# Hybrid trunk kernel: selection and adaLN steps held back during the spatial gating, and another block order in the first layer's attention

## The chip, the cores and the metric

One core of a Trainium2 chip runs the whole kernel. The metric is the device time of one execution in microseconds. All times below are of the kernel before; the trace is that of one profiled execution.

## The reference

Two layers of a decoder trunk for one sequence of 1024 tokens with a width of 1024. Each layer normalises its input and modulates it by adaLN, multiplies it by one wide input matrix, and splits the product: u, v and z_a feed a spatial gating unit (group A), q, k, val and z_b a sparse attention (group B), and q_idx, k_idx and w_idx an indexer that scores which 256 keys each query may see.

```
def hybrid_layer(x, cond, cos, sin, w_ada, ...):
    mod = cond @ w_ada + b_ada
    shift, scale, gate = jnp.split(mod, 3, axis=-1)
    h = layer_norm(x) * (1.0 + scale[:, None, :]) + shift[:, None, :]
    proj = h @ w_in
    u, v, z_a, q, k, val, z_b, q_idx, k_idx, w_idx = jnp.split(proj, SPLIT_POINTS, axis=-1)
    y_a = jax.nn.silu(z_a) * spatial_gating_unit(u, v, v_norm_g, v_norm_b, w_spatial, b_spatial)
    # rope on q, k, q_idx, k_idx
    y_b = jax.nn.silu(z_b) * sparse_attention(q, k, val, q_idx, k_idx, w_idx)
    y = jnp.concatenate([y_a, y_b], axis=-1) @ w_out
    return layer_norm(ALPHA * x + gate[:, None, :] * y, ln_g, ln_b)

def spatial_gating_unit(u, v, g_v, b_v, w_s, b_s):      # chunks of 128 tokens, 8 groups
    vn = layer_norm(v, g_v, b_v)
    mixed = einsum('gts,bcsgd->bctgd', causal(w_s), vn) + b_s
    return u * mixed

def block(i):                                           # sparse attention, 128 queries
    score = sum over heads of w_idx * relu(q_idx . k_idx), causal
    idx = top_k(score, 256)
    p = softmax(q . k[idx] * scale), valid keys only
    return p @ v[idx]
```

## The kernel before

**Numbers and tiles.** All is float32. A matmul is done as three: each operand is split into a high and a low part, and high x high, low x high and high x low are summed in PSUM. Tokens lie in eight blocks of 128 (0 to 7), and in two halves of 512 (blocks 0 to 3 and 4 to 7). A scheduler sorts the instructions of each engine beforehand: what is written earlier in the program has priority, and later work that is ready fills gaps. So each engine runs a fixed row of instructions, and the order in which generators are advanced in the code sets where they stand in it.

**A layer, in the order of the code.** `layer` (L876 on) projects keys and values and the first half of the indexer's queries, and then goes through a list of weight pairs, n = 0 to 10 (L883 to L889): the indexer's second pair of queries, two pairs of v, two of q, and then u and z_a twice each, and two of z_b. The projections are L349. `halves` (L882) says which half of the tokens is projected first: blocks 0 to 3, or blocks 4 to 7 where the layer before treated a block from 4 up first.

**Behind n = 0** the indexer's scores of blocks 2 to 7 are made (L528 to L538, the last addition being the causal mask L538), and `select` is put into the list of generators (L935). It finds for each row of a block the threshold of the 256 best by bisection: statistics of the scores (L556, L557), then six rounds. A round counts the scores over a threshold for six blocks (L543, six counts with 384 to 1024 columns), and updates the bounds with some ten small operations (L584 to L600). Behind the rounds stand a sum on TensorE (L606), a flag, a branch that is hardly ever taken (L612), and per block the masks (L621 to L629). Blocks 0 and 1 need no selection.

**Behind n = 2** comes the spatial gating `sgu` (L468): for each of eight chunks four transposes of v (L474), its statistics (L234, L236, L238, and a power on GpSimd, L239), the norm (L243), a product with the spatial weights (L442) into the single PSUM buffer "o", and four operations on DVE (L480) that add the bias and write the result. Later u is multiplied on (L492) straight from the projection's PSUM buffer "acc", of which there are two.

**Side work.** `side()` (L910 to L920) is called between the pieces of the projections (from n = 1) and between the chunks of the gating (L938). Each call adds PACE_SEL to one account and PACE to another; for each whole unit the first advances `select` by one step, the second, from n = BACK on, one step of the next layer's adaLN (`ada_step`). Such a step is for instance a scaled addition of 128 rows of the adaLN matrix on DVE (L199; the first of a sum is L197); its sum is closed by matmuls with ones (L213, L223) and additions on DVE (L215, L224). For n under BACK no step is made by side(). What is left when the list is through is drained (L940).

**The attention** (L948 to L999) goes over sixteen steps: each block in the order of ORDERS and each of two groups of four heads. `att_soft` makes scores (L678), adds the mask and finds the maximum on DVE (L679), then exponentials on ScalarE (L684), a reciprocal (L686) and a product on GpSimd (L687). `att_pv` transposes the probabilities (L698), splits them (L701 on ScalarE, L702 on DVE) and multiplies by v (L703, L704) into "o"; L710 and L712 apply the gate. A block's length grows with its number: block 7 has 8 key blocks, block 0 has one. Between the steps the output projection (L740) is filled in: for the order's positions in MERGE both halves of a block's output at once (`merge_top`), for others group A's half ahead (`out_top`) and group B's after (`out_bottom`). The next layer's rows are normalised, transposed (L272) and loaded there, in the attention's order; those of the last blocks behind it (L1000 to L1008). MERGE and TOPS speak of positions in the order, not of block numbers.

Of the kernel before, what the change touches and what calls it, by code (L numbers as in the profile page):

```python
# [66 lines left out]
class Trunk:  # L67
    BUFS = dict(h=16, ya=4, wr=2, w=6, r=6, kd=2, vv=1, q=2, ga=6, gb=3, gc=4)
    PBUFS = dict(acc=2, s=2, pt=3, o=1)
    PACE_SEL = 0.8  # L70
    STEPS = 6
    PTAGS = ('ya', 'w', 'w', 'ya', 'w')
    ORDERS = ((1, 0, 2, 3, 4, 5, 6, 7), (4, 5, 6, 2, 3, 7, 1, 0))
    PACE = 1.1
    RDVE = 1
    DMOD = ()
    RT = 2
    XK = (0, 4, 4, 7)
    H0 = 10
    BACK = 5  # L80
    ADAE = (1, 1, 1)
    ADA0 = 0
    ADA1 = 0
# [678 lines left out]
    def bottom_split(self, l, A):  # L762
        A["r"] = self.load_row(self.xin[l] if self.ORDERS[l].index(A["i"]) in self.MERGE[l] else self.r_dram[l], A["i"])
        A["ys"] = self.g("gc", [P, 4, P], F32R), self.g("gc", [P, 4, P], F32R)
        self.split(A["ys"][0], A["ys"][1], A["y"])
# [8 lines left out]
    def out_bottom(self, l, A, w, end):  # L774
        nc = self.nc
        i, r = A["i"], A["r"]
        for nh in range(2):
            acc = yield from self.out_mm(w, A["ys"], nh, A["acc"][nh])
            rv = r[:, nh * 512:(nh + 1) * 512]
            if self.ORDERS[l].index(i) in self.MERGE[l]:  # L780
                nc.vector.scalar_tensor_tensor(rv, rv, ALPHA, acc, op0=ALU.mult, op1=ALU.add)  # L781
# [94 lines left out]
    def layer(self, l, wts):  # L876
# [4 lines left out]
        self.ya = []  # L881
        self.halves = (0, 1) if l == 0 or self.ORDERS[l - 1][0] < 4 else (1, 0)  # L882
        specs = [(C_QI + 256, True, lambda w: self.queries(l, 1, 1, w))]  # L883
# [11 lines left out]
        def ada_step(k):  # L895
            while k and back:
                if next(back[0], 1):
                    back.pop(0)
                else:
                    k -= 1  # L900
# [9 lines left out]
        def side():  # L910
            owed[0] += self.PACE_SEL
            while owed[0] >= 1:
                owed[0] -= 1
                for g in gens:
                    next(g, None)
            owed[1] += self.PACE
            while owed[1] >= 1:
                owed[1] -= 1
                if n >= self.BACK:
                    ada_step(1)  # L920

        w = self.load_pair(l, specs[0][0], specs[0][1])
        for n, (c0, rope, f) in enumerate(specs):
            nw = self.load_pair(l, specs[n + 1][0], specs[n + 1][1]) if n + 1 < len(specs) else None
            for _ in f(w):
                if n:
                    side()
                if n < self.BACK:
                    ada_step(self.ADA1)
            w = nw  # L930
            if n == 0:
                for i in range(2, NB):
                    masks[i] = self.t(f"sc{i}", [P, (i + 1) * P])
                    self.drain(self.scores(l, i, masks[i]))
                gens.append(self.select(masks, range(2, NB)))  # L935
                self.sgu_setup(l)
            if n == 2:
                for _ in self.sgu(l):  # L938
                    side()
        for g in gens + back:  # L940
            self.drain(g)
        wt, wb = [], []
# [4 lines left out]
        nc.sync.dma_start(self.lb, a["ln_b"][l].partition_broadcast(P))  # L947
        order = self.ORDERS[l]  # L948
        steps = [(i, g) for i in order for g in range(2)]
# [111 lines left out]
```

## Time and profile before

| | |
|---|---|
| median of 3 runs | 1205.03 us (1204.15 to 1211.92) |
| profiled execution | 1208.58 us |
| its span | 1206.9 us, mean granted TensorE clock 0.969 |
| TensorE | 1122.7 us busy (93%), 5460 instructions |
| weight loads | 892.3 us (74%), beside TensorE |
| DVE | 842.1 us (70%), 1900 |
| ScalarE | 502.2 us (42%), 972 |
| GpSimd | 554.7 us (46%), 469 |

Times count from the first instruction of the profiled execution. A row of the waits says which instruction TensorE stood before, who ended the idle time, its sum, its number and the longest. A busy time over a stretch counts only what lies within. In a timeline a run of equal instructions stands in one row with its count, and what it waited for in brackets. The clock is the share of full speed (2.4 GHz) that was granted, mean over a stretch; 0.5 is 1.2 GHz.

### The profile page before, as it was taken

The numbers are of one execution on the slowest core, as the hardware profiler recorded it, in microseconds if no ns is written. First come the engines' busy times: TensorE is split into PE (matmuls) and PEld (weight loads), VectorE is DVE, ScalarE is ACT, GpSimd is POOL, SyncE is SP. The second block draws the span as 40 slices with busy tenths as digits, with TensorE's granted clock in tenths as the row PEclk, the third lists the DMA queues.
The fourth block names the chain that finished last, engine by engine and source line by source line (L and its number), as shares of the span: only waits on it lengthen the run. The fifth ranks groups of instructions, "written<-read, shape, count | busy, mean of one in ns | idle before, by whom it ended". The sixth has DMA issues, their size and how long they took to land. (4 is left out here: it accounts for less than half of the span.)

```text
span 1206.9 us, 16501 instructions
## 1 busy us (share of the span) xinstructions
PE 1122.7 (93%) x5460; PEld 892.3 (74%) x5460; DVE 842.1 (70%) x1900; ACT 502.2 (42%) x972; POOL 554.7 (46%) x469
## 2 busy tenths in 40 slices
PE   5889999997999989988988999999989998999997
PEld 1467788866878778866766787888677886787885
DVE  6775666999773355688985467589977127878775
ACT  0342355420202454465764435562211136667561
POOL 1563310553323495474766532126323357565653
PEclk9989999998899989999999999999989998999999
DMA  8935721567412574322232474222621246132311
GB/s 264 278 101 179 205 71 36 166 219 257 117 54 79 166 218 158 105 97 62 86 95 74 138 229 123 70 68 88 227 90 45 88 132 202 51 106 88 114 36 61
DMA packets 127057, 152.11 MB, mean 126 GB/s; under 512 B 17396, under 2 KB 94580, under 8 KB 126968
## 3 DMA queue, kind: packets, MB, share of 16 engines
q1 hardware_dynamic: 126968, 151.03, 40.4%
q8 instruction: 43, 0.70, 0.2%
q14 instruction: 46, 0.38, 0.1%
HBM read 111.40 MB, written 35.40 MB: 122 GB/s over the span
## 5 line engine op out<-in xcount | busy, mean ns | idle before, releaser
L349 PE MATMUL pacc<-h,w 128*128 128x512 f32 (+2 forms) x2304 | 548.5, 394 | 10.8 <-DVE ya L492 8.4
L349 PEld LDWEIGHTS pacc<-h,w 128*128 128x128 f32 (+1 forms) x2304 | 427.1, 190 | 106.8 <-DVE ya L492 10.1
L303 POOL TENSOR_TENSOR w<-wr,w 128x512 fp32r<-128x512 f32 (+1 forms) x100 | 133.0, 1345 | 247.7 <-ACT w L302 231.9
L740 PE MATMUL pacc<-h,gc 128*128 128x512 f32 x768 | 196.7, 401 | 10.8 <-ACT gc L302 10.8
L740 PEld LDWEIGHTS pacc<-h,gc 128*128 128x128 f32 x768 | 143.8, 192 | 40.0 <-ACT gc L302 11.9
L302 ACT ACTIVATE w<-wr 128x512 fp32r<-128x512 f32 (+1 forms) x100 | 56.4, 601 | 208.9 <-PE pacc L349 147.0
L535 DVE SCALAR_TENSOR_TENSOR sc<-gc,wi,sc 128x384 f32<-128x384 f32 (+3 forms) x140 | 99.3, 752 | 38.8 <-ACT gc L530 37.0
L678 PE MATMUL ps<-kd,q 128*128 128x512 f32 (+4 forms) x384 | 106.2, 377 | 9.1 <-DVE mx L679 8.8
L702 DVE TENSOR_TENSOR ga<-ppt,ga 128x512 fp32r<-128x512 f32 x144 | 96.6, 684 | 15.5 <-ACT ga L701 14.9
L701 ACT ACTIVATE ga<-ppt 128x512 fp32r<-128x512 f32 x144 | 82.4, 592 | 36.8 <-PE ppt L698 35.9
L368 POOL TENSOR_TENSOR ga<-ga,ga 128x512 fp32r<-128x512 f32 (+2 forms) x40 | 56.9, 1429 | 85.5 <-ACT ga L367 76.8
L678 PEld LDWEIGHTS ps<-kd,q 128*128 128x128 f32 x384 | 65.1, 196 | 26.7 <-DVE mx L679 19.5
L687 POOL TENSOR_SCALAR w<-w,rd 128x256 f32<-128x256 f32 (+6 forms) x77 | 61.3, 799 | 50.7 <-DVE rd L686 32.5
L698 PE MATMUL ppt<-ident,w 128*128 128x128 f32 x349 | 74.9, 276 | 0.0
L239 POOL TENSOR_TENSOR rs<-rs,mhalf 128x1 f32<-128x1 f32 x48 | 34.8, 730 | 81.2 <-DVE rs L238 81.2
L722 DVE TENSOR_TENSOR wr<-wr,r 128x1024 f32<-128x1024 f32 x8 | 12.1, 1508 | 84.6 <-DMA wr<-in_w_out 52.3
L684 ACT ACTIVATE w<-w,mx 128x256 f32<-128x256 f32 (+6 forms) x77 | 60.6, 787 | 23.4 <-DVE mx L679 23.1
L703 PE MATMUL po<-ga,vv 128*128 128x512 f32 x144 | 62.4, 433 | 8.5 <-DVE gb L710 6.7
L543 DVE TENSOR_SCALAR_CACHE_REDUCE junkd<-sc,sv 128x384 int8<-128x384 f32 (+2 forms) x72 | 67.7, 940 | 1.4
L704 PE MATMUL po<-ga,vv 128*128 128x512 f32 x144 | 63.2, 439 | 3.0 <-DVE ga L702 2.9
L530 ACT ACTIVATE gc<-ppt 128x384 f32<-128x384 f32 (+3 forms) x96 | 47.9, 526 | 30.4 <-PE ppt L528 25.8
L199 DVE SCALAR_TENSOR_TENSOR r<-r,cond,r 128x1024 f32<-128x1024 f32 x28 | 41.8, 1494 | 25.4 <-DMA r<-in_w_ada 25.4
(198 smaller groups left out, 1750.5 us busy)
## 6 DMA issues: line engine op xcount, KB each, us to landing
wr<-in_w_in SPq DMA_DIRECT2D x50, 512.0 KB, 4.7
r<-in_w_ada SPq DMA_DIRECT2D x32, 512.0 KB, 4.2
q<-q SPq DMA_DIRECT2D x112, 128.0 KB, 3.2
q<-ga SPq DMA_DIRECT2D x48, 256.0 KB, 3.0
h<-in_w_ada SPq DMA_DIRECT2D x32, 256.0 KB, 5.2
wr<-in_w_out SPq DMA_DIRECT2D x16, 512.0 KB, 4.1
r<-r SPq DMA_DIRECT2D x14, 512.0 KB, 3.9
r<-x SPq DMA_DIRECT2D x12, 512.0 KB, 4.8
```

Of the source, the lines that this page charges most:

```text
L303: self.nc.gpsimd.tensor_tensor(lo, src, hi.bitcast(F32), op=ALU.subtract)
L349: self.nc.tensor.matmul(acc[:m, :tn], w[:, k, :m], h[:, k % 2, t0:t0 + tn], start=(k == 0 and i == 0), stop=(k == NK - 1 and i == 2))
L535: nc.vector.scalar_tensor_tensor(sc[:, c0:c0 + w], r[:, :w], wsc, sc[:, c0:c0 + w], op0=ALU.mult, op1=ALU.add)
L543: self.nc.vector.tensor_scalar(j[:, :n], sc, thr, None, op0=op, op1=ALU.add, accum_out=out)
L678: nc.tensor.matmul(ps[:, :w], q[:, g * 4 + h, :], self.KD[x][:, c0:c0 + w], start=(x == 0), stop=(x == 1))
L687: nc.gpsimd.tensor_scalar(pm[:, :n], pm[:, :n], rd, 0.0, op0=ALU.mult, op1=ALU.add)
L698: nc.tensor.transpose(pt[:, h * P:(h + 1) * P], pr[h][:, kt * P:(kt + 1) * P], self.ident)
L701: nc.scalar.activation(ph, pt, AF.Copy)
L702: nc.vector.tensor_tensor(pl, pt, ph.bitcast(F32), op=ALU.subtract)
L703: nc.tensor.matmul(o, self.V[:, kt, :], ph, start=(kt == 0), stop=False)
L704: nc.tensor.matmul(o, self.V[:, kt, :], pl, start=False, stop=(kt == i))
L740: self.nc.tensor.matmul(acc, s[:, k, :], m[:, cs], start=(first and k == i == 0), stop=(not more and k == 3 and i == 2))
```

## The change

PACE_SEL and PACE are raised, so that a call of side() makes more steps; BACK goes from 5 to 6. `side()` is called only for n over 2, and the gating is drained without it. The first layer's attention goes over blocks 4, 5, 6, 7, 2, 3, 1, 0 in place of 1, 0, 2, 3, 4, 5, 6, 7; by L882 the second layer then projects blocks 4 to 7 first. All other tables stay, and with MERGE the first four positions of the first layer's order are now blocks 4 to 7.

```diff
 class Trunk:
-    PACE_SEL = 0.8
+    PACE_SEL = 1.4
+    PACE = 1.5
     STEPS = 6
     PTAGS = ('ya', 'w', 'w', 'ya', 'w')
-    ORDERS = ((1, 0, 2, 3, 4, 5, 6, 7), (4, 5, 6, 2, 3, 7, 1, 0))
-    PACE = 1.1
+    ORDERS = ((4, 5, 6, 7, 2, 3, 1, 0), (4, 5, 6, 2, 3, 7, 1, 0))
...
-    BACK = 5
+    BACK = 6
...
             for _ in f(w):
-                if n:
+                if n > 2:
                     side()
                 if n < self.BACK:
                     ada_step(self.ADA1)
...
             if n == 2:
-                for _ in self.sgu(l):
-                    side()
+                self.drain(self.sgu(l))
```

**The order of instructions, first place: DVE in the first layer's gating.** Names are tile names (ya the gated rows, junkd the selection's scratch, sc a block's scores, gc a chunk's normalised v, bn and mv its statistics, r an adaLN sum). Before, around the first chunk's products:

```order
L236 BN_AGGR mv_1959<-bn_1957 128x2
L543 TENSOR_SCALAR junkd_1910,sv_1812<-sc_280_1284,sv_1812 128x768
L199 SCALAR_TENSOR_TENSOR r_2925<-r_2958,cond_61,r_2925 128x1024
L236 BN_AGGR mv_1990<-bn_1988 128x2
L238 TENSOR_SCALAR rs_1961<-mv_1959 128x1
L543 TENSOR_SCALAR junkd_1939,sv_1812<-sc_314_1387,sv_1812 128x896
L238 TENSOR_SCALAR rs_1992<-mv_1990 128x1
L243 TENSOR_SCALAR gc_1964<-ppt_1952,mv_1959,rs_1961 128x512
L543 TENSOR_SCALAR junkd_1941,sv_1812<-sc_348_1490,sv_1812 128x1024
L480 SCALAR_TENSOR_TENSOR ya_1642<-po_1926,vg_1609,bsum_1613 128x128
```

The same place now:

```order
L199 SCALAR_TENSOR_TENSOR r_2933<-r_2978,cond_61,r_2933 128x1024
L236 BN_AGGR mv_1904<-bn_1902 128x2
L236 BN_AGGR mv_1931<-bn_1929 128x2
L238 TENSOR_SCALAR rs_1906<-mv_1904 128x1
L238 TENSOR_SCALAR rs_1933<-mv_1931 128x1
L234 BN_STATS bn_1956<-ppt_1951 128x6
L236 BN_AGGR mv_1958<-bn_1956 128x2
L238 TENSOR_SCALAR rs_1960<-mv_1958 128x1
L480 SCALAR_TENSOR_TENSOR ya_1642<-po_1884,vg_1609,bsum_1613 128x128
```

The counts L543 have gone from between the chunk's statistics and products; the adaLN addition L199 stands there as before.

**Second place: TensorE where the second layer's gating ends** (po is the buffer "o", q the spatial weights, pacc a projection). Now, around the last three chunks' products:

```order
L349 MATMUL pacc_9697<-h_6699,w_9433 128x512
L349 MATMUL pacc_9697<-h_6703,w_9433 128x512
L349 MATMUL pacc_9697<-h_6699,w_9434 128x512
L442 MATMUL po_9183<-q_8760,gc_9181 64x128 x8
L442 MATMUL po_9210<-q_8760,gc_9208 64x128 x8
L442 MATMUL po_9237<-q_8760,gc_9235 64x128 x8
L349 MATMUL pacc_9727<-h_7591,w_9433 128x512
```

Before, the last two of these groups stood side by side at this place and the sixth stood by itself, projections L349 behind it; now the last three stand in a row.

**Third place: TensorE at the end of the first layer's attention**, behind the last product of the last step (h in L740 is the output weights, gc the attention's result split in two, pacc the output). Before:

```order
L703 MATMUL po_7413<-ga_7496,vv_599 128x512
L704 MATMUL po_7413<-ga_7497,vv_599 128x512
L272 MATMUL ppt_7619<-ident_66,q_7196 128x128
L272 MATMUL ppt_7619<-ident_66,q_7402 128x128
L272 MATMUL ppt_7619<-ident_66,q_7196 128x128
L272 MATMUL ppt_7619<-ident_66,q_7402 128x128
L740 MATMUL pacc_7549<-h_4956,gc_7509 128x512
```

Now:

```order
L703 MATMUL po_7490<-ga_7496,vv_599 128x512
L704 MATMUL po_7490<-ga_7497,vv_599 128x512
L740 MATMUL pacc_7383<-h_4956,gc_7363 128x512
L740 MATMUL pacc_7383<-h_4963,gc_7362 128x512
L740 MATMUL pacc_7383<-h_4964,gc_7362 128x512
```

The transposes L272 that stood behind the last step have gone from here, and output products of the block before follow at once; 44 of them stand between this place and the next layer's first L349.

## Rows read from the trace of the kernel before

**Rows 1.** The page's first part: busy time of each engine.

```profile
PE 1122.7 (93%) x5460; PEld 892.3 (74%) x5460; DVE 842.1 (70%) x1900; ACT 502.2 (42%) x972; POOL 554.7 (46%) x469
```

**Rows 2.** Busy time in stretches: start and end, length, engines, clock, DMA.

```profile
core 0: us, PE busy (x) PEld busy (x) DVE busy (x) ACT busy (x) POOL busy (x), PEclk, DMA share, GB/s
222.90:302.60 79.70, 70.55 (x415) 54.87 (x413) 75.50 (x160) 13.74 (x24) 38.13 (x30) 0.93 0.69 225
...
425.60:522.10 96.50, 94.71 (x455) 78.19 (x455) 63.33 (x173) 49.27 (x105) 62.80 (x60) 0.97 0.47 140
522.10:642.30 120.20, 106.41 (x545) 82.40 (x545) 102.23 (x262) 79.45 (x148) 77.94 (x68) 0.96 0.29 90
817.00:879.50 62.50, 57.42 (x348) 44.71 (x346) 59.99 (x163) 13.00 (x21) 28.56 (x27) 0.99 0.49 160
...
1001.90:1190.20 188.30, 183.68 (x949) 149.56 (x950) 142.46 (x402) 115.97 (x235) 113.51 (x104) 0.99 0.29 92
...
1152.50:1190.20 37.70, 36.32 (x191) 29.77 (x190) 26.12 (x74) 20.79 (x49) 19.89 (x22) 1.00 0.15 50
```

**Rows 3.** TensorE's waits, 222.9 to 302.6: sum, times, longest.

```profile
PE pacc L349 <- DVE ya L492: 2.9, 1, 2.9
PE ppt L213 <- DVE r L199: 2.0, 1, 2.0
PE ppt L474 <- DVE rs L238: 2.0, 1, 2.0
PE po L442 <- DVE ya L480: 1.9, 2, 1.3
```

**Rows 4.** Groups by line, whole span: count, busy, mean ns, idle before.

```profile
L199 DVE SCALAR_TENSOR_TENSOR r<-r,cond,r 128x1024 f32<-128x1024 f32 x28 | 41.8, 1494 | 25.4 <-DMA r<-in_w_ada 25.4
...
L556 DVE BATCH_NORM_STATS2 bn<-sc 128x6 f32<-128x256 f32 x12 | 5.0, 419 | 0.0
...
L557 DVE BATCH_NORM_AGGREGATE smv<-bn 128x2 f32<-128x6 f32 x12 | 2.1, 175 | 0.1
```

**Rows 5.** DVE's timeline: first counts of two rounds. Start, us, instruction.

```profile
302.41 0.61 DVE L543 TENSOR_SCALAR_CACHE_REDUCE junkd<-sc,sv 128x384 int8<-128x384 f32 x1
...
310.41 0.61 DVE L543 TENSOR_SCALAR_CACHE_REDUCE junkd<-sc,sv 128x384 int8<-128x384 f32 x1
```

**Rows 6.** TensorE's waits, 817 to 880.

```profile
PE pacc L349 <- DVE ya L492: 3.8, 2, 3.4
PE po L442 <- DVE ya L480: 1.3, 1, 1.3
```

**Rows 7.** TensorE's timeline, start and end of layer 0's attention.

```profile
425.56 2.08 PE L740 MATMUL pacc<-h,gc 128*128 128x512 f32 x4 [3.10 <-ACT gc L302]
...
643.88 2.08 PE L740 MATMUL pacc<-h,gc 128*128 128x512 f32 x4 [2.63 <-ACT gc L302]
...
651.21 1.98 PE L349 MATMUL pacc<-h,w 128*128 128x512 f32 x8
```

**Rows 8.** Timelines: the selection's last masks, first scores, the eighth step's end.

```profile
372.87 1.22 DVE L629 TENSOR_SCALAR sc<-sc 128x896 f32<-128x896 f32 x2
...
417.25 0.64 PE L678 MATMUL ps<-kd,q 128*128 128x256 f32 x4
...
521.28 0.85 DVE L710 TENSOR_TENSOR gb<-po,ga 64x256 f32<-64x256 f32 x2
```

**Rows 9.** A piece of layer 1's chain, and two transposes from TensorE's timeline.

```profile
922.02 56.07 PE pacc L349 x246
...
1174.40 0.27 PE L698 MATMUL ppt<-ident,ya 128*128 128x128 f32 x1
1174.51 0.38 PE L698 MATMUL ppt<-ident,w 128*128 128x128 f32 x2
```

**Rows 10.** TensorE's waits, 522.1 to 651.2.

```profile
PE ps L678 <- DVE mx L679: 5.5, 9, 2.1
```

## Prediction

> **What bounds the kernel now.** First the busy shares: TensorE works for 1122.7 of 1206.9 us, 93%, DVE for 70% [rows 1], so some 84 us of TensorE's idle time is all that a new order can take back; no work is removed. What counts is where those idle microseconds lie and who ends them, so I cut the span at the stages that the change touches [rows 2]. In the first layer's spatial gating (222.9 to 302.6) TensorE is busy for 70.55 of 79.70 us and DVE for 75.50: DVE is the bound there. TensorE's waits say the same: all four groups, 8.8 us, are ended by DVE [rows 3]. In the second layer's gating (817.0 to 879.5) TensorE lacks 5.1 us and DVE works for 59.99 of 62.50; the waits are again DVE's [rows 6]. The third touched stage is the first layer's attention. I cut it at the end of its eighth step (the DVE product that closes the step, 521.28 + 0.85 = 522.1 [rows 8]; the sixteenth ends at 642.3 in the same way). Its halves are unlike: in the first eight steps (blocks 1, 0, 2, 3) DVE is busy for 63.33 of 96.50 us and TensorE for 94.71; in the last eight (blocks 4 to 7) DVE for 102.23 of 120.20 and TensorE for 106.41 [rows 2]. There the waits are TensorE waiting for DVE's softmax maximum, 5.5 us in nine pieces [rows 10]. So short blocks with the merged output halves load TensorE, long blocks load DVE.
>
> **The gating of layer 0.** Between the last score's mask and the last DVE result that TensorE waits for, both orders hold the same 14 scaled adds L199, two L197, eight chunks' statistics and norms, 18 rotary products and 28 chunk products L480. The adaLN steps have hardly moved: both orders have both sums done before the last chunk, whatever PACE and BACK say. What differs is the selection. Before, two rounds of six counts L543 stand in between; after, one round, with the six statistics pairs L556, L557 that used to lie before the stretch. A round costs 8.00 us on DVE: the first count of one starts at 302.41, of the next at 310.41, with little between that isn't the round's own [rows 5]. Against it stand 6 x 0.419 + 5 x 0.175 = 3.4 us of statistics [rows 4]. DVE's stretch is shorter by 8.0 - 3.4 = 4.6 us, and as DVE is the bound, the stage is too. The bounds: below, nothing, if a stall of u*v L492 (2.9 now, [rows 3]) grows by as much; above, all 8.8 us of TensorE's waits [rows 3]. I take 4.6.
>
> The round that leaves goes behind the gating, where TensorE has projections: layer 1's chain shows 246 of them in 56.07 us without a gap [rows 9]. DVE's rows up to the last mask sum to the same in both orders within 0.5 us, so the selection still ends at 372.87 + 1.22 = 374.1 [rows 8]. Who waits for it changes: block 4 now comes first and needs it, where blocks 1 and 0 didn't. The order holds three pairs of block 4's score products L678 ahead of the attention; the third needs the PSUM buffer of the first, which is free once L679 has read it with the selected mask. That pair stands 98 TensorE rows, 22 us, before the main row of L678, which starts at 417.25 now [rows 8] and some 5 earlier then: 390. Against 374 that leaves 16 us. I cost the move at nothing; past those 16, each microsecond of lateness costs one.
>
> **The gating of layer 1.** Here the scores begin 44 TensorE rows later (10 us at 0.228 each [rows 9]), because the first calls of side() no longer mix selection in, and the gating is packed into 193 TensorE rows in place of 260. DVE's rows there sum to 52.4 us in place of 71.7, so DVE's surplus of work goes into the projections behind. The last three chunks' products L442 then stand in one row, where two did, each waiting for the four L480 of the one before in the single "o" buffer: one wait of 1.3 becomes two [rows 6], 2.6, while the u*v wait of 3.8 goes down with DVE's load, to some 0.4. I put 3.0 us of idle in place of 5.1: 2.1 us gained, between 0 and 5.1.
>
> **The attention of layer 0.** The work stays, all but 5 us of TensorE's that move behind the sixteenth step; its split over the steps changes. Prices: a matmul of 512 columns 56.07 / 246 = 0.228 us, narrower ones in proportion, a transpose 0.11 (two starts lie 0.11 apart, 1174.40 and 1174.51 [rows 9]); DVE by the mean of each form in the lines view. Counted to the end of the eighth step, TensorE's order holds 264 L740 in both, but 78 transposes before and 213 after, 40 and 104 products L703 and L704. The sums, first and second eight:
> before: TensorE 88.2 and 93.7, DVE 75.4 and 102.8;
> after: TensorE 132.1 and 44.8, DVE 112.7 and 59.3.
> Larger of each half: 88.2 + 102.8 = 191.0 before, 132.1 + 59.3 = 191.4 after: on work alone there is nothing to gain. What a half takes above its larger sum is 96.5 - 88.2 = 8.3 (9.4%) and 120.2 - 102.8 = 17.4 (16.9%) [rows 2]. A TensorE-bound first half then takes 132.1 + 8.3 = 140.4 or 132.1 x 1.094 = 144.5, a DVE-bound second 59.3 x 1.169 = 69.3. Total 209.7 or 213.8, mean 211.7, against 216.7: 5.0 less. Behind it stand 44 products of the last output, all on TensorE: 44 x 0.228 + 1.3 to start = 11.3 until layer 1's first projection, against 651.2 - 642.3 = 8.9 now [rows 7], with 2.6 of idle in it. So 2.4 back, net gain 2.6. The start wait of 3.10 for the split weights (L740 at 425.56 [rows 7]) stays. The bounds of this term are rivals B (18 less) and A (29 more).
>
> Layer 1's first projections now take blocks 4 to 7 (half 1) first; the half that is ready last, blocks 0 to 3, is needed 22 us later (96 x 0.228) where it was 17, so I cost it at nothing. Layer 1's attention has the same rows.
>
> **Sum.** -4.6 - 2.1 - 2.6 = -9.3 us. The profiled execution took 1208.58 with 1206.9 of span, so it would become 1199.3; it lies 3.55 above the median of the runs, 1205.03. From the median: 1195.7, said as 1196.
>
> **Rivals.**
> A, slower: the short tail. The last eight steps become blocks 2, 3, 1, 0 with only 44.8 us of TensorE work in them. If each step's chain (scores, maximum, exp, transpose, product) isn't filled, TensorE idles between and its granted clock falls to 1.2 GHz. For it: the first eight steps of now began so: four L740 took 2.08 us at 425.56, 0.52 each, half speed, after 3.10 idle [rows 7]. Against it: layer 1 ends on blocks 7, 1, 0 and has TensorE busy for 36.32 of the last 37.70 us at clock 1.00 [rows 2]. Price: 44.8 x 2 x 1.094 = 98.0 in place of 69.3, that is 28.7 more, 1224. It is slower than before once the eight steps take over 69.3 + 9.3 = 78.6, or 9.8 us each.
> The Trainium skill (TensorE: Matmul & The Clock Gate, section HAM oscillation) says that a matmul stage of short bursts with waits between them is put back to the half clock again and again, and pays for each return. The row at 425.56 agrees with it, the last 37.70 us of layer 1 don't; by that rule alone the tail would take the 98.0.
>
> B, faster: the whole stage behaves like layer 1's attention, which starts with long blocks as well. That takes 188.3 us [rows 2] for 172 us of TensorE's sum by the same prices, 1.095. For it: long blocks early have out_top, out_bottom and next-layer work to fill with. 176.9 x 1.095 = 193.7 in place of 211.7: 18 less, 1178. Against it: layer 0's DVE has 172.0 us of work in these steps, layer 1's 152, so the same ratio is not free.
>
> C, nothing comes of the gating: the adaLN adds stay where they were, DVE is as full as before and a stall only moves from L213 to L492 or to the statistics of the packed chunks. For it: DVE alone has 75.5 of 79.7 us and 28 L199 average 1494 ns [rows 4]; the packed order puts three chunks at a time behind one L199. Then 4.6 and 2.1 are lost: 1202, or 1205 if the attention's 2.6 goes too.
>
> **Chances.** Forecast (1188 to 1201) 0.52, B 0.17, C 0.18, A 0.13. One per cent is about what a measurement of this kernel can tell from no change; faster then means below 1193.0, slower above 1217.1. Of the forecast I put 0.42 under 1193.0, so faster 0.22 + 0.17 = 0.39; slower is A less its milder half-cases, 0.10; the rest, 0.51, is the same. The range: B's upper half and A's mild part in, 1180 to 1212, with some 0.1 left out on each side.
>
> **What would show it.** In the gating of layer 0: DVE's counts L543 there from 12 to 6, the stage 75 us in place of 79.7, TensorE's waits down to some 4. If the stage keeps 79 or more, C. In layer 1's: idle 3 in place of 5.1, with L442 waiting for L480 two or three times. In the attention: first eight steps 140 to 145, last eight about 69, and the clock of the last eight at 0.9 or more; last eight over 79 with a clock under 0.8 is A; the two together under 196 is B. The selection has to end before 390 less what the gating gains, otherwise the 16 us were counted wrong. Layer 1's start: first projection 11 us after the sixteenth step, no wait for half 0. If the sums hold and the time doesn't, the two prices above the sums (8.3 and 16.9%) were the wrong step.

## The result, and the profile after

The changed kernel takes 1217.75 us (median of 15 runs, 1210.92 to 1223.61) against 1208.18 us for the kernel before (15 runs, 1202.07 to 1213.26). The ratio is 1.008, with a 95% interval of 1.0061 to 1.0098: slower by 0.8%, where 1196 us (1180 to 1212) had been forecast. Some 3 us of the miss lie in the starting point: the forecast set out from 1205.03, the median of three runs, and fifteen runs give 1208.18. The profiled execution of the changed kernel took 1214.39 us with a span of 1212.4 us, 5.5 us more than the span before. It is among the faster of its 15, so the stages below account for some six of the ten microseconds.

The page after, first part, answers to [rows 1]: TensorE has 4.6 us less of recorded busy time and 10.1 us more of idle time.

```profile
span 1212.4 us, 16526 instructions
PE 1118.1 (92%) x5460; PEld 889.0 (73%) x5460; DVE 863.5 (71%) x1900; ACT 500.1 (41%) x970; POOL 561.5 (46%) x469
```

I cut both traces at the same events (first score product, last mask, last L480 of the gating, first L740, eighth and sixteenth step, first projection of layer 1, and so on; layer 1's gating begins at the end of its last score product). A single trace is a rough measure: the first stage, up to the first score product, takes 129.8 to 135.1 us in the fourteen traces cut like this. Lengths in us:

| stage | before | after | difference |
|---|---|---|---|
| to the first score product of layer 0 | 131.9 | 130.8 | -1.1 |
| scores of layer 0 | 91.9 | 89.6 | -2.3 |
| gating of layer 0 | 76.4 | 76.0 | -0.4 |
| projections to the first L740 | 125.4 | 125.5 | +0.1 |
| attention of layer 0, steps 1 to 8 | 96.5 | 142.7 | |
| steps 9 to 16 | 120.2 | 79.9 | +5.9 (both halves) |
| to the first projection of layer 1 | 8.9 | 8.8 | -0.1 |
| first projection to first score of layer 1 | 70.1 | 81.0 | |
| scores, gating and projections of layer 1 | 280.6 | 272.7 | +3.0 (with the row above) |
| attention of layer 1, and the rest | 205.0 | 205.4 | +0.4 |

The rows of the stretches after (start and end, length, busy time of the engines with instruction counts, granted clock, DMA), to be held against [rows 2]:

```profile
core 0: us, PE busy (x) PEld busy (x) DVE busy (x) ACT busy (x) POOL busy (x), PEclk, DMA share, GB/s
220.40:296.40 76.00, 68.95 (x408) 53.31 (x406) 69.13 (x148) 13.18 (x24) 37.25 (x30) 0.92 0.73 245
421.90:564.60 142.70, 140.22 (x717) 115.34 (x717) 104.30 (x277) 82.27 (x153) 79.02 (x66) 0.98 0.35 108
564.60:644.50 79.90, 57.52 (x267) 43.55 (x268) 66.39 (x152) 46.74 (x109) 58.02 (x60) 0.83 0.39 123
623.00:640.00 17.00, 3.27 (x8) 1.41 (x7) 15.04 (x6) 4.91 (x9) 15.82 (x16) 0.50 0.52 159
653.30:734.30 81.00, 80.53 (x415) 65.46 (x414) 50.48 (x68) 31.21 (x61) 46.77 (x34) 1.00 0.50 153
820.30:879.00 58.70, 51.67 (x336) 39.42 (x334) 50.82 (x135) 12.37 (x22) 22.62 (x24) 0.96 0.49 158
```

Three things stand out. The first eight steps took what was forecast (140 to 145). The last eight have the clock at 0.83, and from 623 to 640 TensorE does almost nothing, at half clock. In layer 1's gating TensorE's idle time is 58.70 - 51.67 = 7.0 us; over the same cut before it was 69.3 - 65.9 = 3.4:

```profile
808.50:877.80 69.30, 65.92 (x402) 51.33 (x400) 66.58 (x173) 16.92 (x28) 33.16 (x31) 1.00 0.50 162
```

What ends TensorE's waits in the last eight steps and the way to layer 1:

```profile
PE ppt L272 <- DVE q L243: 12.0, 1, 12.0
PE po L704 <- DVE ga L702: 3.5, 4, 1.7
PE po L703 <- DVE gb L710: 2.7, 3, 1.8
PE ps L678 <- DVE mx L679: 1.0, 2, 0.6
```

One wait of 12.0 us has taken the place of the nine in [rows 10]. Its cause is one DVE instruction, the norm of a next-layer row; DVE's timeline has it as

```profile
626.49 12.89 DVE L243 TENSOR_SCALAR q<-q,mv,rs 128x1024 f32<-128x1024 f32 x1 [1.46 <-POOL rs L239]
```

while GpSimd's timeline shows a row of work without a pause, from before the norm to 0.6 us before its end:

```profile
626.45 0.47 POOL L687 TENSOR_SCALAR ya<-ya,rd 128x256 f32<-128x256 f32 x1
626.89 2.33 POOL L795 TENSOR_TENSOR r<-r,r 128x1024 f32<-128x1024 f32 x1
629.20 1.26 POOL L712 TENSOR_TENSOR gb<-gb,gb 128x512 f32<-128x512 f32 x1
...
637.57 1.25 POOL L303 TENSOR_TENSOR gc<-gb,gc 128x512 fp32r<-128x512 f32 x1
```

This looked like the whole loss. The experiments show that it isn't.

### The profile page after: what moved, and what is told of

It is laid out like the page before. It is cut to its first block, busy times and chain, and to the rows that moved or that the text cites. A ratio compares the mean times of both kernels' runs of the same rounds, so it can differ in the third digit from the quotient of the medians.

```text
span 1212.4 us, 16526 instructions
## 1 busy us (share of the span) xinstructions
PE 1118.1 (92%) x5460; PEld 889.0 (73%) x5460; DVE 863.5 (71%) x1900; ACT 500.1 (41%) x970; POOL 561.5 (46%) x469
## 4 chain that ended last, share of the span: by engine, by line
PE 48%; DVE 10%; DMA 4%; issue 3%; POOL 2%; ACT 2%; SPq 1%; DVEq 0%; ACTq 0%; POOLq 0%
PE pacc L349 18%; PE pacc L740 13%; PE ppt L698 4%; PE ps L678 4%; PE po L704 3%; PE po L703 2%; PE ppt L528 1%; DVE q L243 1%; POOL h L725 1%; DMA gc<-ya 1%; DMA wr<-in_w_out 1%; SPq L109 1%; DVE sc L535 1%; PE ps L528 1%; DVE gb L710 1%
## 5 line engine op out<-in xcount | busy, mean ns | idle before, releaser
L349 PE MATMUL pacc<-h,w 128*128 128x512 f32 (+2 forms) x2304 | 549.0, 393 | 15.1 <-DVE ya L492 10.1
L349 PEld LDWEIGHTS pacc<-h,w 128*128 128x128 f32 (+1 forms) x2304 | 425.7, 190 | 111.2 <-DVE ya L492 11.1
L303 POOL TENSOR_TENSOR w<-wr,w 128x512 fp32r<-128x512 f32 (+1 forms) x100 | 137.2, 1387 | 270.6 <-ACT w L302 246.1
L740 PE MATMUL pacc<-h,gc 128*128 128x512 f32 x768 | 198.8, 402 | 9.0 <-ACT gc L302 8.8
L740 PEld LDWEIGHTS pacc<-h,gc 128*128 128x128 f32 x768 | 144.0, 192 | 38.6 <-ACT gc L302 9.6
L535 DVE SCALAR_TENSOR_TENSOR sc<-gc,wi,sc 128x384 f32<-128x384 f32 (+3 forms) x140 | 99.3, 752 | 39.1 <-ACT gc L530 36.9
L678 PE MATMUL ps<-kd,q 128*128 128x384 f32 (+4 forms) x384 | 104.0, 371 | 5.2 <-DVE mx L679 4.6
L687 POOL TENSOR_SCALAR w<-w,rd 128x256 f32<-128x256 f32 (+6 forms) x77 | 61.0, 795 | 56.0 <-DVE rd L686 37.5
L687 POOL TENSOR_SCALAR ya<-ya,rd 128x256 f32<-128x256 f32 (+6 forms) x51 | 43.6, 854 | 57.8 <-DVE rd L686 50.5
L543 DVE TENSOR_SCALAR_CACHE_REDUCE junkd<-sc,sv 128x384 int8<-128x384 f32 (+2 forms) x72 | 67.9, 944 | 1.9
L199 DVE SCALAR_TENSOR_TENSOR r<-r,cond,r 128x1024 f32<-128x1024 f32 x28 | 39.9, 1427 | 33.1 <-DMA r<-in_w_ada 33.0
```

What stands on the lines that cost most here:

```text
L303: self.nc.gpsimd.tensor_tensor(lo, src, hi.bitcast(F32), op=ALU.subtract)
L349: self.nc.tensor.matmul(acc[:m, :tn], w[:, k, :m], h[:, k % 2, t0:t0 + tn], start=(k == 0 and i == 0), stop=(k == NK - 1 and i == 2))
L535: nc.vector.scalar_tensor_tensor(sc[:, c0:c0 + w], r[:, :w], wsc, sc[:, c0:c0 + w], op0=ALU.mult, op1=ALU.add)
L543: self.nc.vector.tensor_scalar(j[:, :n], sc, thr, None, op0=op, op1=ALU.add, accum_out=out)
L678: nc.tensor.matmul(ps[:, :w], q[:, g * 4 + h, :], self.KD[x][:, c0:c0 + w], start=(x == 0), stop=(x == 1))
L687: nc.gpsimd.tensor_scalar(pm[:, :n], pm[:, :n], rd, 0.0, op0=ALU.mult, op1=ALU.add)
```

## The experiments

Ratios are to the kernel before, run beside each, with 95% intervals. Two theories stood at first: L, that the time is lost in the 12.89 us of that norm, which the block order causes; and S, that it is lost by the steps that are held back.

**The two parts apart.**

```diff
 # e1: the changed kernel
-    ORDERS = ((4, 5, 6, 7, 2, 3, 1, 0), (4, 5, 6, 2, 3, 7, 1, 0))
+    ORDERS = ((1, 0, 2, 3, 4, 5, 6, 7), (4, 5, 6, 2, 3, 7, 1, 0))
 # e2: the kernel before
-    ORDERS = ((1, 0, 2, 3, 4, 5, 6, 7), (4, 5, 6, 2, 3, 7, 1, 0))
+    ORDERS = ((4, 5, 6, 7, 2, 3, 1, 0), (4, 5, 6, 2, 3, 7, 1, 0))
```

> The changed kernel with the first layer's old block order 1, 0, 2, 3, 4 to 7: only the selection and adaLN steps are held back. Theory L (the time is lost in one DVE instruction, the norm L243 of a next-layer row, which took 12.89 us beside a row of GpSimd instructions at the end of the first layer's attention, and the new block order puts it there): no L243 over 3 us, time 1205 to 1210, that is within 0.3% of before (before in 15 runs: 1208.18). Theory S (the held back steps cost: TensorE's idle in the second layer's gating went from 3.4 to 7.0 us): 1212 to 1218.

Measured: 1206.96 us, ratio 0.9987 (0.9962 to 1.0012). The steps alone change nothing that can be measured.

> The kernel before with the first layer's new block order and nothing else. Theory L: an L243 over 8 us at the end of the first layer's attention with TensorE idle behind it, time 1211 to 1217. Theory S: no such instruction, the attention 5 us shorter as forecast, 1200 to 1206.

Measured: 1221.67 us, ratio 1.0117 (1.0079 to 1.0155). The order alone costs at least as much as the whole change; the two intervals overlap, so more than that can't be said. Theory S falls. There is an L243 of 12.88 us here too, but the time lies above theory L's range as well.

**The norm taken off DVE.**

```diff
-            self.rows[b] = self.ln_row(self.load_row(self.xin[l], b, tag), 1)
+            self.rows[b] = self.ln_row(self.load_row(self.xin[l], b, tag), 2 if tag == "q" else 1)
```

> The changed kernel, with the norms of the last two next-layer rows (tag q) on ScalarE (L252, L253) in place of DVE's L243; the result is the same sum. Theory L: the 12 us wait of TensorE's L272 goes, the last eight steps take some 68 us in place of 79.9, time 1204 to 1208, 0.8 to 1% under the changed kernel (1217.75). Theory S: unchanged, 1215 to 1220. A third way: GpSimd's row of work keeps another DVE instruction (a copy L283 or an L702) waiting, and half of it comes back.

> The kernel before with the same two norms on ScalarE: a control. There the six L243 of this form took 0.80 to 0.81 us, so moving them should bring or cost under 2 us by both theories: 1206 to 1210. If it gains 5 us or more, the gain of the same edit on the changed kernel is no proof of the 12 us wait.

Measured: on the changed kernel 1219.01 us, ratio 1.0087 (1.0061 to 1.0114); on the kernel before 1209.17, ratio 1.0005 (0.9981 to 1.003). The 12 us wait is gone from e3's trace, and the time hasn't moved. So theory L falls as the account of the loss. What TensorE waits for in e3's last eight steps and the way to layer 1:

```profile
PE po L704 <- DVE ga L702: 4.0, 4, 2.2
PE po L703 <- DVE gb L710: 3.3, 4, 1.8
PE pacc L740 <- POOL gc L303: 3.2, 1, 3.2
PE ppt L272 <- DVE ga L702: 2.5, 1, 2.5
```

The waits have moved on to others, one of them put down to GpSimd (the low part of the last result, L303). From the eighth step to layer 1's first projection e3 takes 72.5 + 13.4 = 85.9 us, the changed kernel 79.9 + 8.8 = 88.7: three come back there.

**Layer 1's start.** In all kernels with the new order layer 1 lost time as well, and this had not been in either theory. Theory H: with blocks 4 to 7 projected first, 48 more projections run ahead of layer 1's first scores and are then missing beside the gating.

```diff
 # e7: the changed kernel
-        self.halves = (0, 1) if l == 0 or self.ORDERS[l - 1][0] < 4 else (1, 0)
+        self.halves = (0, 1)
 # e8: the changed kernel
-        for c in range(NB):
+        for c in [4 * h + x for h in self.halves for x in range(4)]:
```

> The changed kernel, but the second layer projects blocks 0 to 3 first, as before the change. Theory H (half of the loss is there: with blocks 4 to 7 first, 48 more projections, 11 us, run ahead of the first scores, and are missing as filling beside the gating, whose idle went from 3.4 to 7.0 us and in the kernel with the order alone to 9.5): the first scores start some 70 us after the first projection in place of 81, and the gating's idle falls to 3 or less; but the first projection has to wait for blocks 2, 3, 1, 0, so that TensorE idles before it, 10 us or more, and the time is 1212 to 1225. Rival: the idle in the gating stays at 7, it comes from the selection's packed steps.

Measured: 1224.88 us, ratio 1.0132 (1.0099 to 1.0165). Slower in total, as expected, and the two sides can be read apart. Its way to the first projection, its start and its gating:

```profile
641.40:673.50 32.10, 16.74 (x74) 14.11 (x74) 21.92 (x36) 9.76 (x19) 21.27 (x17) 0.75 0.27 89
673.50:741.90 68.40, 68.40 (x345) 54.52 (x343) 33.42 (x45) 20.93 (x42) 25.72 (x21) 0.99 0.48 141
827.50:894.60 67.10, 65.91 (x403) 51.07 (x401) 62.51 (x155) 16.84 (x28) 32.38 (x31) 1.00 0.41 132
```

The start falls from 81.0 to 68.4 us. In the gating stand 403 matmuls in place of 336, and its idle time falls from 7.0 to 67.10 - 65.91 = 1.2 us. Layer 1 from its first projection to its attention takes 342.6 us, 11.1 less than in the changed kernel (353.7). It is paid for with 32.1 us, half of them idle, before the first projection, which waits for the blocks that came last. Theory H holds: the eight kernels that project blocks 4 to 7 first all have a wait of 2.4 to 2.6 us before the gating's first L442; the six that project blocks 0 to 3 first have none.

> The changed kernel with the gating's chunks in the order of the halves, 4 to 7 first in the second layer. If chunks 0 to 3 are late because their half is projected second, the gating starts earlier, its idle falls from 7.0 to under 4 and the time by 3 us or more, to 1214. If the gating waits for DVE's scores, as theory H has it, nothing changes: 1215 to 1220.

Measured: 1215.56 us, ratio 1.0054 (1.0037 to 1.0071), an interval that meets the changed kernel's. The gating's idle time is 5.8 us. The order of the chunks is not what delays it: DVE's first statistics of the gating (L234) start 0.2 us behind the last score's mask, at 830.23 behind 830.01 in e8 and at 826.54 behind 826.33 in the changed kernel, so that DVE takes the gating up when it is through with the scores.

**What bounds the last eight steps.** Theory G says GpSimd's row of work; theory A says that the steps are too short to cover their own chain of dependent work, so that TensorE idles and loses its clock. "Last eight and handover" is the time from the end of the eighth step to layer 1's first projection.

```diff
 # e9: e3, and in out_bottom
-            nc.gpsimd.tensor_tensor(r, r, self.lg, op=ALU.mult)
-            nc.gpsimd.tensor_tensor(r, r, self.lb, op=ALU.add)
+            eng = nc.vector if l == 0 and self.ORDERS[0].index(i) >= 4 else nc.gpsimd
+            eng.tensor_tensor(r, r, self.lg, op=ALU.mult)
+            eng.tensor_tensor(r, r, self.lb, op=ALU.add)
 # f6: the changed kernel
-    ORDERS = ((4, 5, 6, 7, 2, 3, 1, 0), (4, 5, 6, 2, 3, 7, 1, 0))
+    ORDERS = ((4, 5, 6, 7, 1, 0, 2, 3), (4, 5, 6, 2, 3, 7, 1, 0))
 # g3: the changed kernel, in load_pair for the next layer's first weights
-                               lo[j][:, ks, :].rearrange("p k (h d) -> p k h d", h=4), rv)
+                               lo[j][:, ks, :].rearrange("p k (h d) -> p k h d", h=4), rv,
+                               nc.vector if l and tag == "ya" else None)
 # f7: the changed kernel
-    FL = 16
+    FL = 17
```

> The changed kernel with the two norms on ScalarE as in e3, and the products and additions L795, L796 of the first layer's output rows, positions 4 and up, on DVE in place of GpSimd (up to eight instructions of 2.35 us each). Theory G (GpSimd's queue is the bound at the end of the first layer's attention: its row of work from 618 to 639 held DVE, and without that the last output product waits 3.2 us for GpSimd's split L303): the last eight steps and the way to the first projection take under 80 us together (88.7 in the changed kernel, 85.9 in e3), the time falls to 1209 to 1213. Rival (the short blocks' chain of dependent steps is the bound): 84 us or more with GpSimd idle between, time 1215 to 1220.

Measured: 1223.86 us, ratio 1.0118 (1.0083 to 1.0153), above both ranges. Last eight and handover take 71.3 + 12.2 = 83.5 us, between the two ranges, but 37 more products stand ahead of the cut here than in the changed kernel; all sixteen steps and the handover take 233.7 us, where the changed kernel takes 231.4. The work taken from GpSimd was put on DVE, so a gain on one side and a loss on the other can't be told apart. The waits at the end are now other ones:

```profile
PE pacc L740 <- ACT gc L302: 7.1, 2, 6.2
PE po L703 <- DVE gb L710: 6.3, 5, 2.0
PE ppt L698 <- POOL w L687: 3.4, 1, 3.4
```

> The changed kernel with the first layer's order 4, 5, 6, 7, 1, 0, 2, 3: the same blocks in the last eight steps, but the two shortest, 1 and 0, are not the very last. Theory A (the last steps are too short to cover their own chain, so that TensorE idles and falls to half clock): the last eight steps and the way to layer 1's first projection take 83 us or less (87 to 89 in the changed kernel and its variants), time 1209 to 1214. Theory G (GpSimd's queue there is the bound): the same work, 86 or more, 1215 to 1220.

Measured: 1222.32 us, ratio 1.0108 (1.0085 to 1.0131); last eight steps and handover 75.5 + 12.5 = 88.0 us. Theory A had asked for 83 or less. That the two shortest blocks are the very last isn't the point either, and A doesn't hold in that form.

> The changed kernel with four subtractions L303 on DVE in place of GpSimd: the low parts of the second layer's first query weights, which stand in GpSimd's row of work at the end of the first layer's attention (4 of some 1.25 us). Theory G (there the last output's low part waits behind GpSimd's row, 4.7 us of TensorE's idle in e8): last eight steps and handover 83 us or less, time 1210 to 1214. If the bound is the chain through DVE, as the loss in e9 suggests: 86 or more, 1215 to 1222.

> The changed kernel with the loading and splitting of the second layer's first weights issued one step later (FL 17 in place of 16), behind the last step's own work. Theory G: GpSimd's row at the end gets shorter, the last eight steps fall to 70 us or less, but the first projection waits for its weights, 3 to 8 us: 1214 to 1222. If GpSimd's row isn't the bound, the last eight steps stay at 72 or more and the wait is added: 1220 to 1228.

Measured: g3 1221.53 us, ratio 1.011 (1.0062 to 1.0159), last eight and handover 81.1 + 10.0 = 91.1 us; f7 1220.56 us, ratio 1.0092 (1.0064 to 1.0121), 73.0 + 13.9 = 86.9 us. Taking work from GpSimd in three ways brought nothing: theory G falls as a single cause. What stays is that the seven kernels which end on short blocks and can be cut there (after, e2, e3, e8, f6, g3, f7) spend 86 to 91 us, with TensorE's waits put down to DVE, ScalarE and GpSimd in turn, at a clock of 0.83 to 0.95 in the last eight steps. A milder theory A, in which several short chains take turns, would fit that, but no run shows it (a filling of the steps by other work wasn't tried), and one resource as the bound can't be named. What bounds the end stays open.

**Long blocks last.**

```diff
 # f9: the changed kernel (g1: the kernel before, with the same order)
-    ORDERS = ((4, 5, 6, 7, 2, 3, 1, 0), (4, 5, 6, 2, 3, 7, 1, 0))
+    ORDERS = ((2, 3, 1, 0, 4, 5, 6, 7), (4, 5, 6, 2, 3, 7, 1, 0))
```

> The changed kernel with the order 2, 3, 1, 0, 4, 5, 6, 7: long blocks last, layer 1 projects blocks 0 to 3 first. If the two costs of the new order are its short end and the 48 projections that run ahead of layer 1's scores, both are gone and the time is that of the kernel with the steps alone, 1204 to 1209; the 31 us between first projection and scores' end are not needed for it. If the cost is in starting with other blocks than 1 and 0, it stays over 1212.

> The kernel before with the first layer's order 2, 3, 1, 0, 4, 5, 6, 7 and nothing else (steps, PACE, BACK as before). The kernel with this order and the changed steps took 1199.31. If the gain of 9 us comes from the order alone, this one takes 1198 to 1202; if the steps and the order each bring a part (the steps alone brought 0.1%), 1201 to 1204; if the gain needs both, 1205 or more.

Measured: f9 takes 1199.31 us, ratio 0.9932 (0.9912 to 0.9953), faster than both kernels and below the 1204 to 1209 expected; g1 1206.02, ratio 0.9964 (0.9938 to 0.999). By what was said ahead of g1, 1205 us or more meant that the gain needs both parts, and 1206.02 lies there. The product of the parts, 0.9987 x 0.9964 = 0.9951, lies just within f9's interval, so that they simply add up isn't excluded either. f9's handover, layer 1's start and layer 1's gating, and below them e1's start and gating:

```profile
635.60:643.20 7.60, 6.15 (x29) 4.96 (x30) 3.19 (x7) 4.35 (x8) 4.94 (x4) 1.00 0.40 130
643.20:713.30 70.10, 69.28 (x359) 55.99 (x358) 43.75 (x65) 25.83 (x51) 33.11 (x29) 1.00 0.51 152
798.40:865.50 67.10, 65.85 (x402) 51.00 (x400) 62.63 (x155) 16.85 (x28) 30.69 (x31) 1.00 0.41 132
...
655.60:726.60 71.00, 69.52 (x359) 56.09 (x358) 43.11 (x65) 26.21 (x52) 33.12 (x28) 1.00 0.51 150
814.70:881.90 67.20, 65.92 (x403) 51.12 (x401) 62.52 (x155) 16.91 (x28) 32.46 (x31) 1.00 0.41 132
```

The start is back at 70.1 us and the gating's idle at 1.2. Where blocks 0 to 3 come first, the held back steps do shorten layer 1's gating, by about the 2.1 us forecast: 69.3, 69.0 and 69.0 us with the old steps (before, e4, g1), 67.2, 67.1 and 67.1 with the new ones (e1, e7, f9). Over the whole way from the first projection to the attention this is less clear: 350.7, 346.7 and 351.5 us with the old steps, 346.3 (e1) and 344.2 (f9) with the new ones. With blocks 4 to 7 first it takes 352.9 to 358.0 in eight kernels. Why g1's order gains over 1, 0, 2, 3 at all wasn't tried further.

**The gating of layer 0.**

```diff
-            w = self.ada_load(l, grp, k, tag)
+            w = self.ada_load(l, grp, k, tag) if k % 2 == 0 else w
```

> The changed kernel with only every second row block of the adaLN matrix loaded, and used twice (so the second layer's modulation is another; all other work is the same). DVE in the first layer's gating waits 3.4 us for these loads, where it waited for none before the change. If this new wait ate the 4.6 us of selection that left the stage, the gating falls from 76.0 us to 70 to 72 and the time by 4 to 8 us, to 1210 to 1214; if the stage is bound otherwise, it stays at 75 to 77 and the time falls by under 3.

Its modulation of the second layer sent that layer's selection into the exact branch, which is hardly ever taken, so its time (1517.78 us) says nothing and only the first gating is read: 73.6 us in place of 76.0 (76.0 to 80.2 in the ten kernels with the new steps and all loads), and DVE still waits 2.8 us for loads, in place of 3.4. Inconclusive: the wait was not taken away, and about half of the expected gain came.

**The 12.89 us by itself.**

> The kernel before, followed by a probe (work that the output doesn't need): one DVE instruction of the norm's form (128x1024, one SBUF input, two scalars) starts while GpSimd runs 0, 1, 2, 4 and 8 instructions of 128x1024 back to back; then 4 of them beside a scalar_tensor_tensor with two SBUF inputs, beside bn_stats with one, and beside the norm's form cut into four of 256 columns. Theory L (DVE waits for the whole row of GpSimd's instructions): some 0.8 us at 0, then the length of the row, about 1.2, 3.5, 8 and 17 us. Rival: DVE waits for the running instruction alone, at most 2.4 us at any count. bn_stats should keep 0.7 us.

> The kernel before, followed by a second probe that the output doesn't need: GpSimd runs eight instructions of 128x512 on alternating output tiles, so that each can start the moment the one before ends, and one DVE instruction of 128x1024 in the norm's form starts after 1 to 5 small DVE instructions, 0.19 us apart; then a scalar_tensor_tensor, a copy of 512 columns and bn_stats. If DVE can lose the port to one GpSimd instruction after another (as the 12.89 us suggest), one or more of the five take over 4 us; if a free border always lets it in, all take 0.8 to 2.2 us, and the 12.89 us need another cause. bn_stats 0.7 us.

Measured: the norm's form took 0.81 us alone and 1.35 us beside any number of GpSimd instructions:

```profile
1206.48 0.81 DVE L830 TENSOR_SCALAR r<-r,pbc,pbb 128x1024 f32<-128x1024 f32 x1
1208.09 1.35 DVE L830 TENSOR_SCALAR r<-r,pbc,pbb 128x1024 f32<-128x1024 f32 x1
...
1221.85 1.35 DVE L830 TENSOR_SCALAR r<-r,pbc,pbb 128x1024 f32<-128x1024 f32 x1
```

The 0.81 is that with none, the first and the last 1.35 those with one and with eight. By the timelines it got in after the first of them. Cut into four of 256 columns it took 6.87 us, about as long as the four GpSimd instructions beside it; bn_stats kept its 0.69. In the second probe the longest was 2.40 us, a scalar_tensor_tensor. So a wait for the whole row isn't the rule. But in the kernels the same norm took 12.89 (the changed kernel and f10), 12.88 (e2), 6.82 (g3), 4.51 (f7) and 0.98 us (e7 and e8). Each time it started 0.04 to 0.06 us behind the same GpSimd instruction (an L687 of 0.47 us), with a gapless row after it:

```profile
630.00 0.98 DVE L243 TENSOR_SCALAR q<-q,mv,rs 128x1024 f32<-128x1024 f32 x1 [1.57 <-POOL rs L239]
...
628.92 4.51 DVE L243 TENSOR_SCALAR q<-q,mv,rs 128x1024 f32<-128x1024 f32 x1 [0.87 <-POOL rs L239]
```

(the first of e8, the second of f7). It ended 0.54 to 0.60 us behind a border between two of GpSimd's instructions: the first in e8, the third in f7, the fourth in g3, and in the changed kernel and e2 only the end of the row. What decides at a border stays open.

## Why the prediction was wrong

**The step that failed most: "Layer 1's first projections now take blocks 4 to 7 (half 1) first ... so I cost it at nothing".** I looked at whether the late half would be ready in time (it was: TensorE idles 0.5 us in the 81.0 us of the start) and not at what the longer start takes from later. The 11 us of projections that now stand ahead of the scores are the filling that the gating had. The prediction had the numbers, 44 rows later and 193 rows in place of 260, but put the first down to the calls of side(), which no longer mix selection in. That was the wrong cause: e1 makes the same calls, and its start takes 71.0 us and its gating holds 403 matmuls; with the order alone (e2) the start takes 81.6 us and the gating holds 336. Both come from the half. TensorE's waits in layer 1's gating, from 820.3 to 879, which answer to [rows 6]:

```profile
PE po L442 <- DMA gc<-in_v_norm_b: 2.6, 1, 2.6
PE po L442 <- DVE ya L480: 1.6, 1, 1.6
PE po L442 <- DVE sh L587: 1.3, 1, 1.3
```

The first stands before the product of the gating's setup, which needs a loaded row (v_norm_b) in one of the "gc" buffers that the scores use too. The load is issued when DVE's L535 frees a buffer, 4.0 us behind the last score product in place of 2.3, and takes 3.9 us to land; TensorE has 5.5 us of other work until then, where it had 6.6 before and didn't wait. The other two stand ahead of the last two chunks, each just behind the four L480 of the chunk before, in the single "o" buffer: 2.9 us together, where 2.6 was forecast. The u*v wait was forecast to fall from 3.8 to 0.4 us and didn't. It lies just behind the cut; from 820.3 to 882 the same view has it as

```profile
PE pacc L349 <- DVE ya L492: 3.3, 1, 3.3
```

So TensorE idles 7.0 us up to the last L480 and 8.7 with the u*v wait, where 3.0 had been forecast for the 5.1 of before. By themselves the steps kept to the 2.1 us of gain (e1's gating takes 67.2 us, before 69.3), but by luck: there the wait for "o" is gone and the u*v wait is still 2.65 us, the other way round from the forecast. Layer 1 to its attention cost 3.0 us more, not 2.1 less; against e1, which has the same steps, 353.7 - 346.3 = 7.4 more, of which 5.5 are idle time of TensorE, about what the gating alone has more than e1's (7.0 against 1.3), and 1.9 are busy time (the gating's clock is 0.96 in place of 1.00). e7 shows 11.1 for the choice of the half.

**The attention: the first half right, the second too cheap.** 140.4 to 144.5 was forecast for the first eight steps, 142.7 measured. For the last eight 69.3, measured 79.9; with the handover 80.6 against 88.7. The step that failed is the factor 1.169, taken over from the long blocks 4 to 7, where DVE is the bound; in the short ones it isn't (66.39 of 79.90 us, 12 of them a stall). In e3, without the stall, the last eight take 72.5 us and the handover 13.4. Rival B's 193.7 us for all sixteen steps was further off still (222.6). Rival A had its place right, and its point of decision: "over 78.6". Its price of 98.0 was too high: the clock was 0.83 and not one half over the whole, nor under the 0.8 that was its sign. It fell three times. From 623 to 640 it was 0.50, and in two shorter stretches 0.66, each behind 5 us in which TensorE was busy for under 3:

```profile
584.60:589.60 5.00, 5.00 (x21) 3.94 (x22) 3.75 (x12) 2.50 (x7) 5.00 (x5) 0.66 0.17 68
604.60:609.60 5.00, 5.00 (x22) 4.39 (x22) 2.82 (x9) 3.66 (x9) 5.00 (x5) 0.66 0.00 0
```

The Trainium skill (TensorE: Matmul & The Clock Gate, section HAM oscillation) says that waits between bursts put TensorE back to the half clock again and again. These rows agree with it. The table's loss of 5.9 us in the attention is also a difference of two single executions. Kernels that end on the long blocks took 225.6 to 230.6 us there with the handover (before, e4, e1, g1; mean 228.6) and f9 220.6; the eight that end on short blocks and go on with blocks 4 to 7 took 228.5 to 233.7 (mean 230.7). The trace of before is at the low end of its kind, and against e1 the changed kernel loses 0.8 us here and 7.4 in layer 1.

**The gating of layer 0: forecast 4.6, come 0.4 in the stage and 2.3 ahead of it.** Counts L543 went from 12 to 7 (6 had been forecast), and DVE's busy time fell from 72.34 to 69.13 us over the same cut, but the stage kept its 76 us. DVE, which before waited for none of the adaLN loads there, now does:

```profile
DVE r L199 <- DMA r<-in_w_ada: 3.4, 4, 2.3
DVE gc L243 <- POOL rs L239: 1.9, 2, 1.4
```

and TensorE's wait for u*v has grown from 2.9 [rows 3] to 6.8 us, here from 220.4 to 299.2, of which 3.6 lie behind the stage:

```profile
PE pacc L349 <- DVE ya L492: 6.8, 2, 3.6
```

Rival C had said that a stall would move to L492; it did. The wrong step was "as DVE is the bound, the stage is too": DVE's sum was within some 4 us of the stage, and the next limit as near. That the loads are this limit is argued from the waits; f10 didn't settle it. Nor is the stage shorter in any other trace with the new steps: it takes 76.0 to 80.2 us in ten, 74.2 to 76.4 in four with the old ones. From the first score to the first L740 (290.6 to 298.0 us with the new steps, 291.2 to 293.7 with the old) no gain is to be seen.

**What held.** The adaLN steps hardly moved: 14 L199 and two L197 stand in the gating before and after. The selection ended some 6 us later than forecast (last mask at 380.1 in place of 374.1), and still in time: TensorE waited for none of it. The steps' part is worth nothing or a little (e1: 0.9987). In the terms of the forecast's sum the traces give -2.6 (layer 0 to the attention) + 5.8 (attention and handover) + 3.0 (layer 1) - 1.1 + 0.4 = +5.5 us, which is the stage table added up and no second proof.

## What to carry to other kernels

Work that is free to fill gaps is a stock: what one stage uses earlier is missing in a later one, so a changed order has to be priced at the stage that loses its filling, not only at the one that waits. Of the orders tried here, those that end on the long blocks and finish first the half that the next layer projects first did best: 2, 3, 1, 0, 4, 5, 6, 7 with the new steps, and the old order, which does both too, next to it. And the longest single wait of a trace need not be the loss: take it away before believing it.

## What the runs showed of the hardware

A DVE instruction of 0.81 us that starts beside a gapless row of GpSimd instructions can take up to 12.89 us, and the same instruction in like kernels 0.98, 4.51, 6.82 or 12.88. The Trainium skill (SBUF — State Buffer, section Who interferes with whom) says that, for a DVE instruction in a mode that uses both port pairs, the shared pair goes to whichever of the two engines issues first, for the whole instruction, and that the other blocks. The probe's 1.35 us agrees with that; the 12.89 us, in which DVE lost at eight borders, do not follow from it.
